# Gate rows fetched from DRAM by broadcast reads, and the row term of a decay exponent given as an activation's bias

## The chip, the cores and the metric

The kernel runs on one core of a Trainium2 chip. The metric is device time in microseconds (us); three timed runs of the kernel before gave 1290.67, 1292.27 and 1293.1, median 1292.27. The trace and its page come from one more execution, taken by the hardware profiler. Engines are named as the profile names them: PE (TensorE matmul), PEld (TensorE weight load), DVE (VectorE), ACT (ScalarE), POOL (GpSimd), SP (SyncE, which here only issues DMAs); ACTq and SPq are the sequencers of ACT and SP, where DMAs are issued.

## The reference, cut to what matters

One transformer-like layer over 1024 tokens of width 1024: an input projection, two mixers side by side, an output projection, a SwiGLU FFN and a gated extra input. The change concerns the second mixer (mLSTM, four heads, chunks; the kernel uses 128 tokens for a chunk). With `ig` and `lf` the input gate and log forget gate, each one number per token and head, the step of a chunk is, cut down:

```python
g = jnp.cumsum(lf, axis=-1)
dmat = g[..., :, None] - g[..., None, :] + ig[..., None, :]     # [t, s], s <= t
m_inter = g + m_st[..., None]
m_t = jnp.maximum(m_inter, jnp.max(dmat, -1))
w_intra = jnp.exp(dmat - m_t[..., None])
w_inter = jnp.exp(m_inter - m_t)
qk = jnp.einsum('bhtd,bhsd->bhts', q_, k_) * w_intra
num = qk @ v_ + w_inter[..., None] * (q_ @ C_st)
```

The exponent of `w_intra` is a sum of a number that depends on s alone (`ig - g` at s) and one that depends on t alone (minus a running maximum at t). With s on partitions and t along a row, the first is one number per partition, and the second is one row that all partitions share. `w_inter` too is one row per head, by which q (head dimension on partitions, t along the row) is multiplied.

## The kernel before

Every large product is made of three fp32r products of split operands (helper `mm3`, lines 86, 87 and 88); the split is a CAST on ACT (line 81) and a subtraction on DVE (line 82). PE does them one after another through the whole kernel.

The stretch that the change touches is early. After a first pass over x (`tok`), four tiles of the convolution (`f_tile(8 + j, conv_evac)`, j = 0 to 3) are multiplied, each in two halves b = 0 and 1 of 24 products of 512 columns into a PSUM bank `ft`. There are two `ft` banks, so a half can only start when ACT has emptied the bank of the half before the last one: `upad<-ft` at line 368. Behind it come four DVE operations (lines 370 and 372), then a Silu on ACT (line 374) and a DMA.

Meanwhile the gates are prepared with 32 rows (8 chunks x 4 heads) on partitions: `ar` is the number per s, `mc` the running maximum per t, `mt` and `wi` further gate rows (lines 288 to 322). To bring row t of a head to all 128 partitions, the kernel before lets PE do it. `stacked` splits a row into a high and a low half, 64 partitions together. For each of the 8 chunks, DVE makes `rd` (line 337), PE makes two products of 512 columns and 64 rows into a bank `pd` (lines 340 and 341), whose sum is the whole exponent; DVE takes the minimum with the causal mask into `Eall` (line 343) and ACT takes one Exp of 128x512 (line 344). In `mlstm(c)`, four products of 64 rows and 128 columns (line 430, `pw`) spread `wi` over 64 partitions each, from where `qw` (line 431) and `wold` (line 432) read it. The small tiles share three banks `ml`.

The chunks of the mLSTM (`mlstm`, a generator) and of the other mixer (`hgrn`) are advanced in steps (`pump`) between the products of the projection tiles. The order on each engine is set by the framework's scheduler, not by the order of the code alone: products of `pd` stand between products of `ft`. Each engine runs its own list in order; a DMA waits at the head of SP's or ACT's list until what it reads is there. The weights are loaded through SP (`wraw`, two buffers).

Of the kernel before, what the change touches and what calls it, by code (L numbers as in the profile page):

```python
# [18 lines left out]
P = 128  # L19
# [15 lines left out]
NH = NC * 4  # L35
# [13 lines left out]
@with_exitstack  # L49
def block_kernel(ctx, tc, a, out):  # L50
    g = Ctx()
    g.tc, g.nc, g.a, g.out = tc, tc.nc, a, out
    nc = tc.nc
    g.act, g.dve, g.pool, g.pe, g.sp = nc.scalar, nc.vector, nc.gpsimd, nc.tensor, nc.sync

    consts = ctx.enter_context(tc.tile_pool(name="consts", bufs=1))
    dram = ctx.enter_context(tc.tile_pool(name="dram", bufs=1, space=DRAM))
    xt = ctx.enter_context(tc.tile_pool(name="xt", bufs=4))
    mp = ctx.enter_context(tc.tile_pool(name="mp", bufs=16))

# [12 lines left out]

    def big(name):
        return xt.tile([P, KT, HB], F32R, tag="big", bufs=4, name=name)

    def mtile(name):
        return mp.tile([P, HB], F32, tag="m", bufs=16, name=name)

    def split(hi, lo, raw):  # L80
        g.act.copy(hi, raw)  # L81
        g.dve.tensor_sub(lo, raw, hi.bitcast(F32))  # L82

    def mm3(acc, lhs, rhs, first, last, more=False):
        (lh, ll), (rh, rl) = lhs, rhs
        g.pe.matmul(acc, lh, rh, start=first, stop=False, skip_group_check=more)  # L86
        g.pe.matmul(acc, lh, rl, start=False, stop=False, skip_group_check=more)  # L87
        g.pe.matmul(acc, ll, rh, start=False, stop=last, skip_group_check=more)  # L88

    def weights(pool_, width, nraw, nhl):  # L90
        def wtile(src, n=1024):
            raw = pool_.tile([P, width], F32, name="wraw", bufs=nraw)
            g.sp.dma_start(raw[:, :n], src)
            hl = pool_.tile([P, 2, width], F32R, name="whl", bufs=nhl)
            hi, lo = hl[:, 0], hl[:, 1]
            split(hi[:, :n], lo[:, :n], raw[:, :n])
            return hi, lo
        return wtile

    g.const, g.big, g.mtile, g.split, g.mm3, g.weights = const, big, mtile, split, mm3, weights  # L100
    g.m8 = consts.tile([P, 8], F32)
    g.dve.memset(g.m8, -0.5)

    def ln_rows(y, p_):
        st = p_.tile([P, 2, 6], F32, name="st6")
        for s in range(2):
            g.dve.bn_stats(st[:, s], y[:, s * HB:(s + 1) * HB])
        mv = p_.tile([P, 4], F32, name="mvs")
        g.dve.bn_aggr(mv[:, 0:2], st)
        ve, rs = mv[:, 2:3], mv[:, 3:4]  # L110
        g.dve.tensor_scalar(ve, mv[:, 1:2], LN_EPS, None, op0=OP.add)
        g.pool.tensor_tensor(rs, ve, g.m8[:, :1], op=OP.pow)
        g.dve.tensor_scalar(y, y, mv[:, 0:1], rs, op0=OP.subtract, op1=OP.mult)

    g.ln_rows = ln_rows
    g.mix = {}
    g.mp = mp
    with tc.tile_pool(reuse_waits="tile", name="wp", bufs=3) as wp:
        g.wp = wp
        g.wtile = weights(wp, 1056, 2, 3)  # L120
        with ExitStack() as es:
            mixers(g, es)
        ff = ExitStack()
        g.psC = ctx.enter_context(tc.tile_pool(reuse_waits="tile", name="psC", bufs=8, space=PSUM))
        g.fw = ff.enter_context(tc.tile_pool(reuse_waits="tile", name="fw", bufs=3, side="right"))
        g.fh = ff.enter_context(tc.tile_pool(reuse_waits="tile", name="fh", bufs=3, side="right"))
        g.fe = ff.enter_context(tc.tile_pool(reuse_waits="tile", name="fe", bufs=8, side="right"))
        with ExitStack() as es:
            out_proj(g, es)
    with ff:  # L130
        with ExitStack() as es:
            ffn_up(g, es)
    with ExitStack() as es:
        ffn_down(g, es)


def mixers(g, es):
# [6 lines left out]
    def bank(tag, shape, name):  # L144
        return ps.tile(shape, F32, tag=tag, bufs={"ft": 2, "hg": 3, "ml": 3}[tag], name=name)
# [23 lines left out]
    for k in range(KT):  # L169
        kk, q = divmod(k, 4)  # L170
# [108 lines left out]
    def srow(nm, dt=F32, n=NH):  # L279
        return kc.tile([n, P], dt, name=nm)  # L280

    ones = srow("ones", n=2 * NH)
    dve.memset(ones, 1.0)
    pgt = bank("ml", [P, 2, P], "pg")
    for i, nm in enumerate(("ig", "lf")):
        pe.transpose(pgt[0:NH, i], sm[nm].rearrange("p c h -> p (c h)"), ident)
    gg, ar, mc, mt, wi = (srow(nm) for nm in ("gg", "ar", "mc", "mt", "wi"))
    dve.tensor_tensor_scan(gg, ones[0:NH], pgt[0:NH, 1], 0.0, op0=OP.mult, op1=OP.add)
    dve.tensor_sub(ar, pgt[0:NH, 0], gg)
    dve.tensor_tensor_scan(mc, ar, ar, NEG, op0=OP.max, op1=OP.max)  # L290
    pl = bank("ml", [P, 2, NH], "pl")
# [13 lines left out]
    dve.tensor_scalar(mprev[:, 1:2], mc[:, P - 1:P], -1.0, None, op0=OP.mult)  # L305
    dve.tensor_add(mt, gg, mc)

    def stacked(nm, src, neg):
        t2 = kc.tile([2 * NH, P], F32R, name=nm)
        if neg:  # L310
            dve.tensor_scalar(t2[0:NH], src, -1.0, None, op0=OP.mult)
            dve.scalar_tensor_tensor(t2[NH:], src, -1.0, t2[0:NH].bitcast(F32), op0=OP.mult, op1=OP.subtract)
        else:
            dve.tensor_copy(t2[0:NH], src)
            dve.tensor_sub(t2[NH:], src, t2[0:NH].bitcast(F32))
        return t2

    m2 = stacked("m2", mc, True)
    a2 = stacked("a2", ar, False)
    act.activation(mt, mt, AF.Exp, scale=-1.0)  # L320
    act.activation(wi, mc, AF.Exp, bias=mprev[:, 0:1], scale=-1.0)
    act.activation(ar, ar, AF.Exp, bias=mprev[:, 1:2], scale=1.0)
    w2 = stacked("w2", wi, False)
    pc = bank("ml", [P, 2, NH], "pc")
    for i, src in enumerate((ar, mt)):
        pe.transpose(pc[:, i], src, ident[0:NH, 0:NH])
    cols = kc.tile([P, 2, NH], F32)
    dve.tensor_copy(cols, pc)
    eyer = kc.tile([2 * NH, NH], F32R)
    dve.tensor_copy(eyer, eye[0:2 * NH])  # L330
    onesr = srow("onesr", F32R, 2 * NH)
    dve.tensor_copy(onesr, ones)
    Eall = kc.tile([P, NC, 4, P], F32)
    for c in range(NC):
        cc = slice(4 * c, 4 * c + 4)
        rd = mx.tile([2 * NH, 4, P], F32R, name="rd", bufs=1)
        dve.tensor_mul(rd, m2.bitcast(F32)[:, None, :].to_broadcast([2 * NH, 4, P]),
                       eye[0:2 * NH, cc, None].to_broadcast([2 * NH, 4, P]))
        pd = bank("ml", [P, 4, P], "pd")
        pe.matmul(pd, a2, eyer[:, cc, None].to_broadcast([2 * NH, 4, P]), start=True, stop=False)  # L340
        pe.matmul(pd, onesr, rd, start=False, stop=True)
        E = Eall[:, c]
        dve.tensor_tensor(E, pd, causal[:, None, :].to_broadcast([P, 4, P]), op=OP.min)
        act.activation(E, E, AF.Exp)

    nfb = kc.tile([P, 4], F32)
    dve.tensor_scalar(nfb, fbias[:, 0:4], -1.0, None, op0=OP.mult)
# [69 lines left out]
    def mlstm(c):  # L417
# [2 lines left out]
        v = mx.tile([P, 4, VW], F32, name="mv")  # L420
        sp.dma_start(v[:, :, 0:P], g.mv_d[c].rearrange("p (h d) -> p h d", h=4))
        dve.memset(v[:, :, P:VW], 1.0)
        pw = bank("ml", [P, 2, 2, P], "pw")
        qw = mx.tile([P, 2, P], F32, name="qw", bufs=1)
        wold = mx.tile([P, 2], F32, name="wold")
        for q in range(2):
            pr = slice(64 * q, 64 * q + 64)
            for p in range(2):
                hc = 4 * c + 2 * p + q
                pe.matmul(pw[:, q, p], eyer[:, hc:hc + 1].to_broadcast([2 * NH, P]), w2, start=True, stop=True)  # L430
            dve.scalar_tensor_tensor(qw[pr], qk[pr, 0:2], 0.125, pw[pr, q], op0=OP.mult, op1=OP.mult)
            dve.tensor_copy(wold[pr], pw[pr, q, :, P - 1])
        E = Eall[:, c]
        for q in range(2):
            pr = slice(64 * q, 64 * q + 64)
# [6 lines left out]
        for p in range(2):  # L442
            pe.transpose(pk[:, p], qk[:, 2 + p], ident)
        kws = mx.tile([P, 4, 64], F32, name="kws", bufs=1)
        dve.tensor_mul(kws, pk.rearrange("p a (b d) -> p (a b) d", b=2),
                       cols[:, 0, 4 * c:4 * c + 4, None].to_broadcast([P, 4, 64]))
        yield
        views = []
        den = mx.tile([P, 4], F32, name="den")
# [10 lines left out]
        for q in range(2):  # L460
            pn = pns[q]
            dn = den[:, q::2]
            dve.tensor_max(dn, pn[:, :, P], cols[:, 1, 4 * c + q:4 * c + 4:2])
            dve.scalar_tensor_tensor(dn, pn[:, :, P], -1.0, dn, op0=OP.mult, op1=OP.max)
            views.append((slice(q, 4, 2), pn[:, :, 0:P]))
        dve.reciprocal(den, den)
# [694 lines left out]
```

## Time and profile before

| | us |
|---|---|
| median of three timed runs | 1292.27 |
| the profiled execution, whole time | 1293.18 |
| its span, first to last instruction | 1291.4 |
| PE busy | 1272.6 (99%) |
| DVE busy | 870.3 (67%) |
| ACT busy | 445.7 (35%) |
| DMA, mean | 148 GB/s |

Between the span and the whole time lie 1.8 us in which the profile shows no instruction. A matmul's bar in the trace is longer than the distance to the next matmul's start, since matmuls are pipelined: the cost of one is read from start to start, not from the length of its bar. A busy share of 99% therefore hides small delays between products.

### The profile page before, as it was taken

Reading aid. Unit: us, or ns where it says so; the run is one execution under the profiler, and the core shown is the slowest. Engines: PE = TensorE matmul, PEld = TensorE weight load, DVE = VectorE, ACT = ScalarE, POOL = GpSimd, SP = SyncE. Lnnn points to the kernel's source line nnn. Section 1 sums busy time; section 2 is a strip of 40 time slices with the busy share of each in tenths; the row PEclk is TensorE's granted clock in tenths of the full one; section 3 lists DMA queues with packets and bytes.
Section 4 is the critical chain, followed back from the end, with each engine's and each line's share of the span. In section 5 each row is a group of like instructions: output and inputs, shape, how many; then the busy total and the mean of one; then the engine's idle time right before and its main releaser. Section 6 shows DMA issues by size and latency. Waiting matters only on the chain.

```text
span 1291.4 us, 19316 instructions
## 1 busy us (share of the span) xinstructions
PE 1272.6 (99%) x7842; PEld 1050.6 (81%) x7842; DVE 870.3 (67%) x1475; ACT 445.7 (35%) x632; POOL 28.4 (2%) x38
## 2 busy tenths in 40 slices
PE   9999999999999999999999999999999999999998
PEld 8689888877788787787788888888888888888887
DVE  7763666466732654478887787787767884559965
ACT  4631312233322514373333333333323433434141
POOL 0000000000000000000000000000000000000000
PEclk9999999999999999999999999999999999999999
DMA  7244321210111745524644433543538876654432
GB/s 246 79 129 130 99 75 34 75 42 26 52 33 49 262 178 179 204 93 146 211 158 175 159 146 143 188 178 123 188 114 308 320 254 198 216 180 153 172 132 74
DMA packets 86472, 191.17 MB, mean 148 GB/s; under 512 B 8304, under 2 KB 26608, under 8 KB 80624
## 3 DMA queue, kind: packets, MB, share of 16 engines
q1 hardware_dynamic: 52112, 130.95, 30.2%
q10 hardware_dynamic: 34272, 59.00, 12.3%
q8 instruction: 61, 1.00, 0.3%
q14 instruction: 27, 0.22, 0.1%
HBM read 139.32 MB, written 50.59 MB: 147 GB/s over the span
## 4 chain that ended last, share of the span: by engine, by line
PE 92%; DVE 5%; ACT 1%; issue 1%; POOL 1%; DMA 0%; ACTq 0%; SPq 0%; POOLq 0%
PE ft L86 8%; PE ft L87 7%; PE ft L88 7%; PE z L86 3%; PE z L88 3%; PE z L87 3%; PE x L86 3%; PE x L88 3%; PE x L87 3%; PE y L86 3%; PE y L88 3%; PE y L87 3%; PE dna L87 2%; PE dna L86 2%; PE pg L86 2%; PE pg L88 2%
## 5 line engine op out<-in xcount | busy, mean ns | idle before, releaser
L86 PE MATMUL ft<-xh,whl 128*128 128x512 f32 x320 | 129.8, 406 | 1.0 <-ACT k L503 1.0
L88 PE MATMUL ft<-xh,whl 128*128 128x512 f32 x320 | 127.8, 399 | 0.0
L87 PE MATMUL ft<-xl,whl 128*128 128x512 f32 x320 | 127.4, 398 | 0.0
L82 DVE TENSOR_TENSOR whl<-hw,whl 128x2048 fp32r<-128x2048 f32 (+1 forms) x42 | 88.4, 2107 | 54.9 <-ACT whl L81 54.9
L81 ACT CAST whl<-hw 128x2048 fp32r<-128x2048 f32 (+1 forms) x42 | 74.2, 1771 | 116.9 <-PE dna L88 41.4
L82 DVE TENSOR_TENSOR whl<-wraw,whl 128x1024 fp32r<-128x1024 f32 x62 | 75.2, 1219 | 40.7 <-ACT whl L81 40.5
L81 ACT CAST whl<-wraw 128x1024 fp32r<-128x1024 f32 x62 | 64.7, 1051 | 107.9 <-PE wo L88 43.8
L81 ACT CAST hl<-gu 128x1024 fp32r<-128x1024 f32 (+1 forms) x48 | 46.8, 981 | 82.9 <-PE x L88 66.9
L86 PEld LDWEIGHTS ft<-xh,whl 128*128 128x128 f32 x320 | 60.8, 190 | 15.7 <-ACT k L503 1.5
L88 PEld LDWEIGHTS ft<-xh,whl 128*128 128x128 f32 x320 | 60.1, 188 | 14.4 <-issue 1.8
L87 PEld LDWEIGHTS ft<-xl,whl 128*128 128x128 f32 x320 | 60.2, 188 | 12.0 <-issue 0.7
L86 PE MATMUL x<-XS,hl 128*128 128x512 f32 x176 | 68.6, 390 | 0.6 <-DVE p L873 0.6
L86 PE MATMUL z<-XA,hl 128*128 128x512 f32 x176 | 68.7, 390 | 0.0
L87 PE MATMUL x<-XS,hl 128*128 128x512 f32 x176 | 68.5, 389 | 0.0
L88 PE MATMUL x<-XS,hl 128*128 128x512 f32 x176 | 68.5, 389 | 0.0
L87 PE MATMUL z<-XA,hl 128*128 128x512 f32 x176 | 68.5, 389 | 0.0
L88 PE MATMUL dna<-whl 128*128 128x512 f32 x176 | 68.5, 389 | 0.0
L86 PE MATMUL dna<-whl 128*128 128x512 f32 x176 | 68.5, 389 | 0.0
L87 PE MATMUL dna<-whl 128*128 128x512 f32 x176 | 68.5, 389 | 0.0
L88 PE MATMUL z<-XA,hl 128*128 128x512 f32 x176 | 68.0, 389 | 0.0
L82 DVE TENSOR_TENSOR hl<-gu,hl 128x1024 fp32r<-128x1024 f32 (+1 forms) x48 | 54.2, 1133 | 7.2 <-ACT hl L81 7.2
L81 ACT CAST hl<-tt 128x1024 fp32r<-128x1024 f32 (+1 forms) x44 | 36.9, 838 | 55.7 <-PE w L88 26.7
(304 smaller groups left out, 3079.9 us busy)
## 6 DMA issues: line engine op xcount, KB each, us to landing
gu<-in_wgu SPq DMA_DIRECT2D x26, 1024.0 KB, 4.9
hw<-h_d SPq DMA_DIRECT2D x35, 512.0 KB, 4.1
wdp<-in_wd SPq DMA_DIRECT2D x11, 1024.0 KB, 5.0
h_d<-hs ACTq DMA_DIRECT2D x44, 256.0 KB, 3.6
wraw<-in_wf SPq DMA_DIRECT2D x20, 512.0 KB, 3.6
hw<-w_d SPq DMA_DIRECT2D x20, 512.0 KB, 4.9
w_d<-wdp ACTq DMA_DIRECT2D x33, 256.0 KB, 3.5
wraw<-in_wo SPq DMA_DIRECT2D x16, 512.0 KB, 3.4
```

The source lines that it names most:

```text
L81: g.act.copy(hi, raw)
L82: g.dve.tensor_sub(lo, raw, hi.bitcast(F32))
L86: g.pe.matmul(acc, lh, rh, start=first, stop=False, skip_group_check=more)
L87: g.pe.matmul(acc, lh, rl, start=False, stop=False, skip_group_check=more)
L88: g.pe.matmul(acc, ll, rh, start=False, stop=last, skip_group_check=more)
```

## The change

Two small DRAM tensors are added. ACT's queue writes the 32x128 rows `wi` and the negated `mc` there. A helper `spread` issues DMAs on SP that read a row with a step of 0 over the partitions, so that each partition gets the same row. `Eall` of a chunk is loaded so with four rows (512 numbers on each of 128 partitions); DVE adds the causal mask; ACT takes the Exp head by head, 128x128 each, with a column of `cols` (the transposed `ar`) as its bias, 32 in all. In `mlstm`, `wb` (two DMAs per chunk, two buffers) replaces `pw`; `qw` becomes one DVE operation over 128 partitions, and `wold` one copy. `stacked`, `rd`, `eyer`, `onesr` and the products at lines 340, 341 and 430 are gone; a third transpose of 32 columns (`pc`) is added.

```diff
+    g.wi_d = dram.tile([NH, P], F32, name="wi_d")
+    g.m_d = dram.tile([NH, P], F32, name="m_d")
...
-    m2 = stacked("m2", mc, True)
-    a2 = stacked("a2", ar, False)
+    pc = bank("ml", [P, 3, NH], "pc")
+    pe.transpose(pc[:, 0], ar, ident[0:NH, 0:NH])
     act.activation(mt, mt, AF.Exp, scale=-1.0)
     act.activation(wi, mc, AF.Exp, bias=mprev[:, 0:1], scale=-1.0)
+    act.dma_start(g.wi_d, wi)
+    dve.tensor_scalar(mc, mc, -1.0, None, op0=OP.mult)
+    act.dma_start(g.m_d, mc)
     act.activation(ar, ar, AF.Exp, bias=mprev[:, 1:2], scale=1.0)
-    w2 = stacked("w2", wi, False)
...
+    def spread(dst, src, r0, rows):
+        ap = [[0, dst.shape[0]], [rows * P, dst.shape[1]], [1, P]]
+        sp.dma_start(dst, bass.AP(tensor=src.tensor, offset=src.offset + r0 * P, ap=ap))
     for c in range(NC):
-        rd = mx.tile([2 * NH, 4, P], F32R, name="rd", bufs=1)
-        dve.tensor_mul(rd, m2.bitcast(F32)[:, None, :].to_broadcast([2 * NH, 4, P]),
-                       eye[0:2 * NH, cc, None].to_broadcast([2 * NH, 4, P]))
-        pd = bank("ml", [P, 4, P], "pd")
-        pe.matmul(pd, a2, eyer[:, cc, None].to_broadcast([2 * NH, 4, P]), start=True, stop=False)
-        pe.matmul(pd, onesr, rd, start=False, stop=True)
         E = Eall[:, c]
-        dve.tensor_tensor(E, pd, causal[:, None, :].to_broadcast([P, 4, P]), op=OP.min)
-        act.activation(E, E, AF.Exp)
+        spread(E, g.m_d, 4 * c, 1)
+        dve.tensor_add(E, E, causal[:, None, :].to_broadcast([P, 4, P]))
+        for h in range(4):
+            act.activation(E[:, h], E[:, h], AF.Exp, bias=cols[:, 0, 4 * c + h:4 * c + h + 1], scale=1.0)
...
-        pw = bank("ml", [P, 2, 2, P], "pw")
+        wb = mx.tile([P, 2, P], F32, name="wb")
+        for q in range(2):
+            spread(wb[64 * q:64 * q + 64], g.wi_d, 4 * c + q, 2)
         qw = mx.tile([P, 2, P], F32, name="qw", bufs=1)
+        dve.scalar_tensor_tensor(qw, qk[:, 0:2], 0.125, wb, op0=OP.mult, op1=OP.mult)
         wold = mx.tile([P, 2], F32, name="wold")
-        for q in range(2):
-            pr = slice(64 * q, 64 * q + 64)
-            for p in range(2):
-                hc = 4 * c + 2 * p + q
-                pe.matmul(pw[:, q, p], eyer[:, hc:hc + 1].to_broadcast([2 * NH, P]), w2, start=True, stop=True)
-            dve.scalar_tensor_tensor(qw[pr], qk[pr, 0:2], 0.125, pw[pr, q], op0=OP.mult, op1=OP.mult)
-            dve.tensor_copy(wold[pr], pw[pr, q, :, P - 1])
+        dve.tensor_copy(wold, wb[:, :, P - 1])
```

The scheduler moves instructions with it. On PE, in the second convolution tile (j = 1, b = 0), the kernel before has `pd` between the products of `ft` from here on:

```order
L326 MATMUL pc<-c_ident,ar 128x32
L326 MATMUL pc<-c_ident,mt 128x32
L340 MATMUL pd<-eyer,a_496 128x512
L341 MATMUL pd<-rd,onesr 128x512
L340 MATMUL pd<-eyer,a_496 128x512
L88 MATMUL ft<-xh,whl 128x512
L86 MATMUL ft<-xh,whl 128x512
L340 MATMUL pd<-eyer,a_496 128x512
```

The changed kernel, at the same place (its lines are shifted: 88 to 90 are `mm3`):

```order
L319 MATMUL pc<-c_ident,ar 128x32
L319 MATMUL pc<-c_ident,mt 128x32
L89 MATMUL ft<-xl,whl 128x512
L90 MATMUL ft<-xh,whl 128x512
L88 MATMUL ft<-xh,whl 128x512
```

All 16 `pd` products are gone from the row of `ft` products, which now runs unbroken to the end of the convolution.

On ACT, the kernel before takes the Exps of `Eall` in groups of one to three, with an emptying of an `ft` bank (`upad<-ft`) between them (here from the gate rows to the second of these emptyings):

```order
L322 ACTIVATE ar<-ar,mprev 32x128
L81 CAST whl<-wraw 128x1024
L374 ACT_TABLE_LOAD
L374 ACTIVATE st<-st 128x512
L344 ACT_TABLE_LOAD
L344 ACTIVATE Eall<-Eall 128x512 x2
L375 DMA mq_d<-st 128x4x128
L368 ACTIVATE upad<-ft,c_fbias 128x512
L344 ACTIVATE Eall<-Eall 128x512 x3
L81 CAST whl<-wraw 128x1024
L344 ACTIVATE Eall<-Eall 128x512
```

The changed kernel, from the same place, has both new writes and then one block:

```order
L317 ACTIVATE ar<-ar,mprev 32x128
L316 DMA m_d<-mc 32x128
L363 ACT_TABLE_LOAD
L363 ACTIVATE st<-st 128x512
L357 ACTIVATE upad<-ft,c_fbias 128x512
L364 DMA mq_d<-st 128x4x128
L83 CAST whl<-wraw 128x1024
L333 ACT_TABLE_LOAD
L333 ACTIVATE Eall<-Eall,cols 128x128 x32
L363 ACT_TABLE_LOAD
L363 ACTIVATE st<-st 128x512
L357 ACTIVATE upad<-ft,c_fbias 128x512
```

All 32 Exps now stand in one piece between two emptyings of `ft` banks (that of j = 1, b = 0, and that of j = 1, b = 1), with a table load and a Silu behind them.

On SP, at the loads of the projection weights, the changed kernel has:

```order
L95 DMA wraw<-in_wf 128x1024 x4
L95 DMA wraw<-in_wt 128x1024
L325 DMA wb<-wi_d 64x2x128 x2
L325 DMA Eall<-m_d 128x512 x8
L325 DMA wb<-wi_d 64x2x128 x2
L95 DMA wraw<-in_wt 128x1024
```

The last load stood directly behind the one of the second row before; it now waits behind twelve reads of the two new tensors.

## Rows read from the trace of the kernel before

**Rows 1.** The page's first part: span and busy time of each engine.

```profile
span 1291.4 us, 19316 instructions
PE 1272.6 (99%) x7842; PEld 1050.6 (81%) x7842; DVE 870.3 (67%) x1475; ACT 445.7 (35%) x632; POOL 28.4 (2%) x38
```

**Rows 2.** PE in two stretches of the convolution (window: its length, PE busy us, matmuls started; granted clock; DMA share and GB/s): three halves with the work of `pd` between them, then three halves without.

```profile
41.00:67.87 26.87, 26.87 (x95) 1.00 0.16 47
67.87:84.60 16.73, 16.73 (x73) 1.00 0.41 124
```

**Rows 3.** PE in order of time (start us, length us, engine, line, operation, output<-inputs, form, count): first products of j = 1, b = 0, then the run around two `pd` products.

```profile
41.02 0.40 PE L86 MATMUL ft<-xh,whl 128*128 128x512 f32 x1
41.34 0.22 PE L301 MATMUL pm<-ones,mrow 1*32 1x1 f32 x2
41.49 0.50 PE L87 MATMUL ft<-xl,whl 128*128 128x512 f32 x1
...
53.84 0.40 PE L88 MATMUL ft<-xh,whl 128*128 128x512 f32 x1
54.16 0.48 PE L340 MATMUL pd<-eyer,a 64*128 64x512 f32 x1
54.58 0.50 PE L86 MATMUL ft<-xh,whl 128*128 128x512 f32 x1
54.91 0.40 PE L87 MATMUL ft<-xl,whl 128*128 128x512 f32 x1
```

**Rows 4.** The same view where `pw` stands: alone between `ft` products (the last product of j = 2, b = 0, the pair, the first of j = 2, b = 1), in a cluster of small products, and split up.

```profile
67.12 0.40 PE L88 MATMUL ft<-xh,whl 128*128 128x512 f32 x1
67.45 0.43 PE L430 MATMUL pw<-w,eyer 64*128 64x128 f32 x2
67.88 0.50 PE L86 MATMUL ft<-xh,whl 128*128 128x512 f32 x1
68.21 0.39 PE L87 MATMUL ft<-xl,whl 128*128 128x512 f32 x1
...
110.15 0.44 PE L430 MATMUL pw<-w,eyer 64*128 64x128 f32 x2
110.43 0.71 PE L438 MATMUL pq<-mqk 64*128 64x128 f32 x8
...
123.63 0.32 PE L430 MATMUL pw<-w,eyer 64*128 64x128 f32 x1
123.66 0.37 PE L438 MATMUL pq<-mqk 64*128 64x128 f32 x1
123.79 0.27 PE L430 MATMUL pw<-w,eyer 64*128 64x128 f32 x1
123.88 0.49 PE L438 MATMUL pq<-mqk 64*128 64x128 f32 x3
```

**Rows 5.** ACT in order of time, the gate rows and the second emptying (in brackets idle time before, and what ended it), and four 128x128 copies without a bias.

```profile
43.27 0.40 ACT L321 ACTIVATE wi<-mc,mprev 32x128 f32<-32x128 f32 x1
43.57 0.29 ACT L320 ACTIVATE mt<-mt 32x128 f32<-32x128 f32 x1
43.77 0.39 ACT L322 ACTIVATE ar<-ar,mprev 32x128 f32<-32x128 f32 x1
44.07 1.03 ACT L81 CAST whl<-wraw 128x1024 fp32r<-128x1024 f32 x1
45.11 1.28 ACT L374 ACT_TABLE_LOAD   x1
46.41 0.63 ACT L374 ACTIVATE st<-st 128x512 f32<-128x512 f32 x1
...
67.16 0.67 ACT L368 ACTIVATE upad<-ft,c_fbias 128x512 f32<-128x512 f32 x1
...
135.68 0.77 ACT L481 COPY mix<-pt 128x128 f32<-128x128 f32 x4 [5.76 <-PE pt L478]
```

**Rows 6.** DVE: when the gate row `mt` is made (timeline), and length of an instruction (ns, least/median/most, first and last start us) at the lines of the mask and of the convolution.

```profile
42.51 0.27 DVE L306 TENSOR_TENSOR mt<-gg,mc 32x128 f32<-32x128 f32 x1
...
L343 DVE TENSOR_TENSOR Eall<-pd,c_causal x8: 676/692/692, 46.6 to 65.9; 128x512 f32<-128x512 f32 x8
...
L372 DVE SCALAR_TENSOR_TENSOR st<-upad,c_convw,st x24: 733/752/753, 36.3 to 89.2; 128x512 f32<-128x512 f32 x24
```

**Rows 7.** DMA issues (queue, count, KB each, median us from issue to landing) and one issue on SP's sequencer (start, length). `btok`, `ln1b` and `ln2g` are rows read from DRAM with a step of 0 over 128 partitions.

```profile
mqk<-mq_d SPq DMA_DIRECT2D x8, 256.0 KB, 2.7
...
ln1b<-in_ln1b SPq DMA_DIRECT2D x1, 512.0 KB, 7.1
ln2g<-in_ln2g SPq DMA_DIRECT2D x1, 512.0 KB, 14.4
...
btok<-in_btok SPq DMA_DIRECT2D x1, 256.0 KB, 4.8
...
c_lbl<-in_lbl SPq DMA_DIRECT2D x1, 4.0 KB, 2.0
...
20.00 0.43 SPq L71 DMA_DIRECT2D c_ln1c<-in_ln1c  x1
```

**Rows 8.** PE in two stretches later in the kernel (columns as in rows 2): one with waits in it, and the one behind it.

```profile
537.00:540.44 3.44, 1.78 (x7) 1.00 0.73 284
540.44:543.86 3.42, 3.42 (x10) 0.50 0.81 302
```

More of the change, by code (lines that the diff above doesn't have):

```diff
@@ L280, in srow @@
         return kc.tile([n, P], dt, name=nm)
-    ones = srow("ones", n=2 * NH)
+    ones = srow("ones")
     dve.memset(ones, 1.0)
@@ L287, in mixers @@
     gg, ar, mc, mt, wi = (srow(nm) for nm in ("gg", "ar", "mc", "mt", "wi"))
-    dve.tensor_tensor_scan(gg, ones[0:NH], pgt[0:NH, 1], 0.0, op0=OP.mult, op1=OP.add)
+    dve.tensor_tensor_scan(gg, ones, pgt[0:NH, 1], 0.0, op0=OP.mult, op1=OP.add)
     dve.tensor_sub(ar, pgt[0:NH, 0], gg)
@@ L306, in mixers @@
     dve.tensor_add(mt, gg, mc)
[L308 to L316, printed above, removed]
-    m2 = stacked("m2", mc, True)
-    a2 = stacked("a2", ar, False)
+    pc = bank("ml", [P, 3, NH], "pc")
@@ L320, in mixers @@
+    pe.transpose(pc[:, 0], ar, ident[0:NH, 0:NH])
     act.activation(mt, mt, AF.Exp, scale=-1.0)
     act.activation(wi, mc, AF.Exp, bias=mprev[:, 0:1], scale=-1.0)
+    act.dma_start(g.wi_d, wi)
+    dve.tensor_scalar(mc, mc, -1.0, None, op0=OP.mult)
+    act.dma_start(g.m_d, mc)
     act.activation(ar, ar, AF.Exp, bias=mprev[:, 1:2], scale=1.0)
-    w2 = stacked("w2", wi, False)
-    pc = bank("ml", [P, 2, NH], "pc")
     for i, src in enumerate((ar, mt)):
-        pe.transpose(pc[:, i], src, ident[0:NH, 0:NH])
@@ L327, in mixers @@
-    cols = kc.tile([P, 2, NH], F32)
+        pe.transpose(pc[:, 1 + i], src, ident[0:NH, 0:NH])
+    cols = kc.tile([P, 3, NH], F32)
     dve.tensor_copy(cols, pc)
[L329 to L332, printed above, removed]
+    def spread(dst, src, r0, rows):
+        ap = [[0, dst.shape[0]], [rows * P, dst.shape[1]], [1, P]]
+        sp.dma_start(dst, bass.AP(tensor=src.tensor, offset=src.offset + r0 * P, ap=ap))
@@ L333, in mixers @@
     Eall = kc.tile([P, NC, 4, P], F32)
     for c in range(NC):
-        cc = slice(4 * c, 4 * c + 4)
-        rd = mx.tile([2 * NH, 4, P], F32R, name="rd", bufs=1)
-        dve.tensor_mul(rd, m2.bitcast(F32)[:, None, :].to_broadcast([2 * NH, 4, P]),
-                       eye[0:2 * NH, cc, None].to_broadcast([2 * NH, 4, P]))
-        pd = bank("ml", [P, 4, P], "pd")
-        pe.matmul(pd, a2, eyer[:, cc, None].to_broadcast([2 * NH, 4, P]), start=True, stop=False)
-        pe.matmul(pd, onesr, rd, start=False, stop=True)
@@ L445, in mlstm @@
         dve.tensor_mul(kws, pk.rearrange("p a (b d) -> p (a b) d", b=2),
-                       cols[:, 0, 4 * c:4 * c + 4, None].to_broadcast([P, 4, 64]))
+                       cols[:, 1, 4 * c:4 * c + 4, None].to_broadcast([P, 4, 64]))
         yield
@@ L462, in mlstm @@
             dn = den[:, q::2]
-            dve.tensor_max(dn, pn[:, :, P], cols[:, 1, 4 * c + q:4 * c + 4:2])
+            dve.tensor_max(dn, pn[:, :, P], cols[:, 2, 4 * c + q:4 * c + 4:2])
             dve.scalar_tensor_tensor(dn, pn[:, :, P], -1.0, dn, op0=OP.mult, op1=OP.max)
```

## The prediction

> **What bounds the kernel now.** I read the page's first part, then windows by stage, then PE's timeline, and last ACT's and DVE's around it. PE is busy for 99% of the span [rows 1], so the time falls only if PE has less to do or waits less; the reader should then distrust the 99%, because bars overlap. The windows show what they hide. Three halves of the convolution without the gate work (67.87 to 84.60) are 16.73 us with 73 matmuls, 0.229 us each; the three halves before them (41.00 to 67.87) hold the same 72 large products and take 26.87 us [rows 2]. So the stretch with `pd` in it is 10.1 us longer. PE's timeline shows how: from the `ft` product at 53.84 to the next at 54.58 it is 0.74 us instead of 0.23, and the one behind needs 0.33, so one `pd` product costs 0.61 us although it computes as many columns as an `ft` product [rows 3]. Switching between 64 and 128 rows costs as much as the work. The 16 of them at 0.61 would be 9.8; as some stand side by side I go by the stretch: 10.1, less 0.6 for the one lone `pw` pair in it (67.12 to 67.88 is 0.76 instead of 0.23, the next start 0.10 late) [rows 4] and some 0.6 for the transposes and `pm` that stay, which leaves 8.9.
>
> **What goes, part by part.** *PE, `pd`:* 8.9 us of PE's list, and 0.6 for the lone `pw` pair. *PE, the other 15 `pw` pairs:* in a cluster a pair holds the products behind it up by 0.28 us (110.15 to 110.43); where the scheduler split it, the two parts hold up 0.03 and 0.09 [rows 4]. Bounds for 15: 1.8 and 4.2, or 9.5 if each cost what the lone one did; I take 0.24 each, near the plain cluster, 3.6 us. PE is the bound there, so this counts in full. *DVE:* `rd`, `stacked` and one of two `qw` operations per chunk go; DVE does not bound here, worth nothing by itself. The mask costs what it did (0.69) [rows 6].
>
> **What comes, and where it decides.** The `ft` products now run unbroken, but each half needs a bank that ACT must empty, and all 32 Exps stand between the emptying of j = 1, b = 0 and that of j = 1, b = 1. So I follow that list.
>
> - PE: j = 1, b = 0 starts at 41.02 as before [rows 3]; 24 products at 0.23 and about 0.8 for `pm` (0.34 from 41.02 to 41.49 beyond a product's distance, less what the first product takes) and three transposes end it near 47.6. The next half needs 5.5 more, the one after that (into the bank emptied near 48.3) ends at 58.7. Its successor, j = 2, b = 1, wants the bank of j = 1, b = 1.
> - The row: `mt` is made at 42.51 to 42.78; then three convolution operations of 0.72 and the negation of 0.27 [rows 6] give `mc` at 45.2. ACT writes it (a small DMA lands after 2.0), SP issues the first `Eall` at 47.3; it lands 2.6 later as `mqk`, 256 KB, does: 49.9 [rows 7]. Eight issues at 0.4 to 0.7 put the last landing near 54. DVE reaches the first mask only after the convolution operations ahead of it: 51.2.
> - ACT: after the write at 45.2 (0.35) a table load 1.28, Silu 0.63, emptying 0.67 (47.6 to 48.3), a DMA issue 0.37, a CAST 1.03, a table load 1.28: ready at 51.0 [rows 5]. Queue, DVE and ACT thus meet within 1.5 us of each other.
> - 32 Exps with a bias: the trace has no 128x128 one. The 32-row ones of the same row length: with a bias they last 0.39 to 0.40, and the next starts 0.30 later (43.27 to 43.57, 43.77 to 44.07); without, 0.29 and 0.20. Four copies without a bias take 0.77, so 0.165 each [rows 5]. Bounds 0.165 and 0.40, that is 5.3 and 12.8 us; I take 0.30, the row with a bias: 9.6. They end at 60.9; DVE's masks (8 x 0.69 and the split of a weight) are done near 58 and don't bind.
> - Then table load 1.28, Silu 0.63, emptying 0.67: the bank is free at 63.5. PE, done at 58.7, waits 4.8 us. Before, j = 2, b = 1 began at 67.88 [rows 4]. Gain here: 4.4 of the 9.5 that left PE's list. The rest waits on ACT.
>
> The queue of SP: what stands behind the broadcasts are the weights of the second `tok_group`, wanted past 80; ACT's and DVE's lists behind the Exps run some 2 us ahead of PE's next need. I count them at nothing; the cover is gone if the Exps end 3 us later. The reads of `wb` wait for the buffer of two chunks earlier, as `mqk` does; nothing.
>
> **The clock.** A wait of this kind has a second price. In a stretch of 3.44 us in which PE was busy for 1.78, the granted clock was still 1.00; in the next 3.42 it was 0.50, that is 1.2 instead of 2.4 GHz, and PE made 10 matmuls in it [rows 8] where 15 fit at 0.229. That is 1.1 to 1.6 us lost. A wait of 4.8 us is longer than the 1.66 idle in that stretch, so I add one such loss, 1.6; bounds are nothing (the low clock lies inside the wait) and two, 3.2. The Trainium skill (TensorE: Matmul & The Clock Gate, Why this matters for your kernels) says the same as a rule: keep PE free of idle gaps between bursts, or its clock falls back to the low level. That rule speaks against this change, and rows 8 bear it out; no wait as long stands in this trace. Without it the sum below would be 1.6 better.
>
> **The sum.** Against the profiled execution, 1293.18 (span 1291.4 and 1.8 around it): 4.4 - 1.6 + 3.6 = 6.4 us less, 1286.8. The median shown is 0.9 under that execution, so the like median is 1285.9; I say 1286.0. Behind the mixers nothing is touched, and PE's list there just starts earlier.
>
> **Rivals.**
> 1. *The block is short, PE does not wait for ACT* (20%). If an Exp starts each 0.165, DVE's masks bind, the block ends near 58.9, the bank is free at 61.5, PE waits 2.8 and the clock may hold: 6.4 + 3.6 = 10.0 less, 1282. For it: the copies in rows 5. Against: the rows with a bias.
> 2. *The block is long or late, the stage gives nothing* (20%). At 0.40 the Exps end at 64.0, the bank at 66.6; with 1.6 to 3.2 for the clock the stage loses 0.3 to 1.9, and `pw` alone is left: 1.7 to 3.3 less, 1289 to 1291. A landing 3 us later does the same. For it: three chains meet within 1.5 us, and any delay of one moves the block. Against: each has its own row.
> 3. *The broadcasts are slow, and the kernel becomes slower* (8%). Rows read with step 0 over the partitions landed 7.1 and 14.4 us after issue for 512 KB, 4.8 for 256 KB [rows 7], up to three times a plain read. If 256 KB each take 3.5 us one after another, eight take 28: the last lands at 75.5, masks, Exps, table, Silu and emptying put the bank at 80, 12 us after 67.88; with the clock 13.7, less 3.6: 10 slower, 1302. It decides once the last row lands after 65, eleven us later than I reckon. Against: those reads stood in line with weight loads, when DMA was far busier than the 47 GB/s of this stretch [rows 2].
> 4. *The change doesn't do what it says* (2%): PE would still hold products at the lines that go. The order excludes it; what is left is any upset of later stages by the new order.
>
> **How the numbers follow.** Forecast 50%, rivals 20, 20, 8, 2. The forecast's own range, from an Exp distance 0.27 to 0.33 and a clock loss of 0 to 3.2, with 0.2 to 0.28 for a `pw` pair, is 1283.5 to 1288.5. To leave out no more than 2 in 10 I go to 1281.5 on rival 1's side and to 1291 on rival 2's. About 0.2% (2.6 us: 1289.7 and 1294.9) is what a measurement can tell. Faster: the forecast, rival 1 and a fifth of rival 2, 0.74; same: the rest of rival 2 and half of rival 4, 0.17; slower: rival 3 and the rest, 0.09.
>
> **What would show it.** In the trace of the changed kernel: no `pd`, no `pw`; `ft` products 0.23 apart from 47 to 58; 32 Exps of some 0.39 us starting each 0.30, first near 51; PE idle for some 5 us before j = 2, b = 1, ended by ACT's `upad`, with a granted clock of 0.5 for about 3.4 us at its end; that half starting near 63.5. If PE does not wait there, rival 1 holds; if the idle time is ended by a landing of `Eall` through DVE, rival 3 or 2. If the stretch from there to the last step of the mLSTM has not become 3 to 4 us shorter, the `pw` term is wrong.

## The result, and the profile after

The changed kernel takes 1283.94 us (median of four runs, 1282.37 to 1285.11), the kernel before 1291.94 in the same comparison: ratio 0.9938, 95% interval 0.9920 to 0.9955, so 8.0 us less. Its profiled execution took 1282.37 us. Two of the four runs took 1282.4 and 1282.8 us at a mean granted clock of 0.998 and 0.997, the other two 1285.1 at 0.995, so they spent longer at the low clock than the execution that the trace shows.

The first part of its page answers to [rows 1]; the last two lines are from the costliest groups and the DMA issues:

```profile
span 1280.6 us, 19251 instructions
PE 1257.1 (98%) x7795; PEld 1043.4 (81%) x7795; DVE 857.4 (67%) x1444; ACT 448.3 (35%) x654; POOL 28.4 (2%) x38
...
L88 PE MATMUL ft<-xh,whl 128*128 128x512 f32 x320 | 129.9, 406 | 5.9 <-ACT upad L357 4.9
...
Eall<-m_d SPq DMA_DIRECT2D x8, 256.0 KB, 5.8
```

PE now has idle time, and one line names it: 4.9 us before an `ft` product, ended by ACT's emptying `upad`. ACT's timeline between the two emptyings (as rows 5) shows what it was doing instead:

```profile
48.04 0.69 ACT L357 ACTIVATE upad<-ft,c_fbias 128x512 f32<-128x512 f32 x1 [0.28 <-PE ft L90]
48.10 0.39 ACTq L364 DMA_DIRECT2D mq_d<-st  x1
48.62 1.04 ACT L83 CAST whl<-wraw 128x1024 fp32r<-128x1024 f32 x1
49.68 1.28 ACT L333 ACT_TABLE_LOAD   x1
51.84 9.56 ACT L333 ACTIVATE Eall<-Eall,cols 128x128 f32<-128x128 f32 x32 [0.87 <-DVE Eall L331]
61.42 1.28 ACT L363 ACT_TABLE_LOAD   x1
62.72 0.63 ACT L363 ACTIVATE st<-st 128x512 f32<-128x512 f32 x1
63.25 0.67 ACT L357 ACTIVATE upad<-ft,c_fbias 128x512 f32<-128x512 f32 x1
```

PE's timeline at that place, and behind it windows of two and four us (window: its length; busy us and instructions of PE, PEld, DVE, ACT and POOL; granted clock; DMA share and GB/s):

```profile
58.70 0.40 PE L90 MATMUL ft<-xh,whl 128*128 128x512 f32 x1
63.97 0.67 PE L88 MATMUL ft<-xh,whl 128*128 128x512 f32 x1 [4.87 <-ACT upad L357]
```

The windows:

```profile
60.00:64.00 4.00, 0.03 (x1) 0.03 (x1) 0.04 (x1) 3.97 (x9) 0.00 (x0) 1.00 0.00 1
64.00:66.00 2.00, 2.00 (x5) 1.62 (x6) 1.93 (x4) 0.86 (x1) 0.00 (x0) 0.54 0.50 139
66.00:68.00 2.00, 2.00 (x7) 1.53 (x7) 1.88 (x4) 0.09 (x1) 0.00 (x0) 0.61 0.00 0
68.00:70.00 2.00, 2.00 (x10) 1.66 (x9) 0.85 (x3) 1.12 (x2) 0.00 (x0) 1.00 0.55 154
```

The clock was granted in full while PE stood still; it fell to 0.50 (1.2 of 2.4 GHz) as PE started again, for 3.41 us (64.14 to 67.55), and PE made 5 and 7 products in windows where it makes 10.

To see where the time went, I compare two places that every kernel of this study has: A, the first 256-column product of the second token group, right behind the convolution, and B, the first `pkt` product, behind the last step of the mLSTM. The median is of the timed runs, and the ratio is to the kernel before timed beside that version (its medians: 1291.65 to 1292.37). A and B are from the traces, one execution each, in us. The first half of the convolution starts between 28.4 and 29.5 in them, so A and B alone carry up to 1.1 us that no edit made; B - A does not:

| kernel | median | ratio, 95% | A | B | B - A |
|---|---|---|---|---|---|
| before | 1291.94 | | 84.63 | 223.80 | 139.17 |
| changed | 1283.94 | 0.9938 (0.9920 to 0.9955) | 82.29 | 215.41 | 133.12 |
| `w_only` | 1287.05 | 0.9962 (0.9950 to 0.9975) | 85.88 | 219.24 | 133.36 |
| `e_only` | 1291.28 | 0.9994 (0.9985 to 1.0003) | 84.46 | 223.59 | 139.13 |
| `pw_dbl` | 1292.82 | 1.0009 (1.0000 to 1.0018) | 84.69 | 225.13 | 140.44 |
| `pw_full` | 1293.20 | 1.0010 (1.0001 to 1.0020) | 84.58 | 224.25 | 139.67 |
| `pw_hg` | 1289.50 | 0.9978 (0.9969 to 0.9987) | 85.13 | 221.21 | 136.08 |
| `fill` | 1281.49 | 0.9920 (0.9907 to 0.9934) | 81.10 | 214.21 | 133.11 |
| `e_late` | 1286.49 | 0.9964 (0.9950 to 0.9977) | 75.82 | 218.92 | 143.10 |
| `exp_one` | 1281.05 | 0.9916 (0.9901 to 0.9930) | 80.11 | 213.32 | 133.21 |
| `exp_in` | 1277.33 | 0.9886 (0.9872 to 0.9901) | 76.56 | 210.25 | 133.69 |

The changed kernel gains 2.34 us to A and 6.05 from A to B; 0.6 is lost again between 257 and 264 us of the kernel before (the gain falls from 8.39 to 7.81; the cause stays open), which leaves 7.8 beside the timed 8.0. The spans differ by 10.8, since the one profiled execution of the kernel before has two delays that are not the change's: at the low clock of [rows 8] the gain steps from 7.78 to 9.35, and at a wait of PE of 1.24 us at 602 to 10.95. The trace of `pw_dbl`, which touches nothing there, has neither; that of `pw_full` has the first.

### The profile page after: what moved, and what is told of

It is laid out like the page before. It is cut to its first block, busy times and chain, and to the rows that moved or that the text cites. A ratio compares the mean times of both kernels' runs of the same rounds, so it can differ in the third digit from the quotient of the medians.

```text
span 1280.6 us, 19251 instructions
## 1 busy us (share of the span) xinstructions
PE 1257.1 (98%) x7795; PEld 1043.4 (81%) x7795; DVE 857.4 (67%) x1444; ACT 448.3 (35%) x654; POOL 28.4 (2%) x38
## 4 chain that ended last, share of the span: by engine, by line
PE 90%; DVE 5%; ACT 2%; issue 1%; DMA 1%; POOL 1%; POOLq 0%; ACTq 0%
PE ft L88 7%; PE ft L89 7%; PE ft L90 7%; PE z L88 3%; PE z L90 3%; PE z L89 3%; PE x L88 3%; PE x L90 3%; PE x L89 3%; PE y L88 3%; PE y L90 3%; PE y L89 3%; PE pg L88 2%; PE dna L89 2%; PE dna L88 2%; PE dna L90 2%
```

## The experiments

### The two parts, each alone

`w_only` is the kernel before with only the `wi` rows read from DRAM; `e_only` is the changed kernel with the `pw` products put back.

```diff
--- before
+++ w_only
...
-        pw = bank("ml", [P, 2, 2, P], "pw")
+        wb = mx.tile([P, 2, P], F32, name="wb")
+        for q in range(2):
+            spread(wb[64 * q:64 * q + 64], g.wi_d, 4 * c + q, 2)
...
--- changed
+++ e_only
...
-        wb = mx.tile([P, 2, P], F32, name="wb")
+        pw = bank("ml", [P, 2, 2, P], "pw")
...
```

> Only the wi rows go through DRAM (wb); the pd products and the Exps of 512 stay as in the kernel before. Theory 1: the two parts of the change add up, and the mLSTM's steps get from this part alone the 6.0 us that the trace of the changed kernel shows between the end of the convolution and the last mLSTM step, besides 0.6 for the lone pw pair in the convolution: about 6 us under the kernel before. Rival: a pw pair costs 0.24 as predicted and the other 2.4 us come from the earlier end of the Exps or of the convolution: about 4 us under, and the mLSTM stretch 3.6 shorter.

> Only Eall is fetched from DRAM, with the bias in the Exp; pw stays. Theory 1: the convolution ends some 2 us earlier than in the kernel before (2.65 less the 0.6 of the lone pw pair), the mLSTM steps take what they took: about 2 us under the kernel before, PE idle for some 5 us before the fourth half of the convolution and a stretch of low clock behind it. Rival: the stage is worth nothing without the other part, 0 us.

Measured: 4.6 us less for `w_only`, 0.4 (not different from nothing) for `e_only`. From A to B, `w_only` alone has 5.81 of the 6.05 us and `e_only` none: the surplus over the forecast belongs to the `pw` part (products, their bank and what reads them). At A `w_only` is 1.25 later, of which 0.27 is its later start; in the convolution PE waits 1.62 us for ACT ahead of j = 2, b = 1. And `e_only` gains nothing there: that half's emptying comes still later (64.89, behind all 32 Exps again), since in its order ACT takes a Silu and a CAST ahead of the block, which starts at 55.53 instead of 51.84. So the rival's 0 us came and not the theory's 2, by the placing of the block; the parts do not simply add up. PE's timeline at these waits, first of `w_only`:

```profile
69.14 0.50 PE L87 MATMUL ft<-xh,whl 128*128 128x512 f32 x1 [1.62 <-ACT upad L373]
```

That of `e_only`, and the window with the low clock:

```profile
58.61 0.43 PE L430 MATMUL pw<-w,eyer 64*128 64x128 f32 x2
65.61 0.80 PE L87 MATMUL ft<-xh,whl 128*128 128x512 f32 x1 [6.57 <-ACT upad L368]
```

```profile
63.39:70.22 6.83, 4.61 (x11) 3.65 (x12) 3.26 (x6) 4.66 (x10) 0.00 (x0) 0.50 0.03 10
```

A wait of 6.57 us, and a low clock for 6.83 us, twice as long as in the changed kernel: all that left PE's list there was given back in one place. Here the clock fell 2.2 us before PE started again (63.39 and 65.61). Behind the wait of `w_only` it stayed at 1.00.

### What a `pw` pair costs

The forecast took a pair by its place in PE's list. Two tests of other prices: each product twice, and the products over 128 rows, half of them zero.

```diff
--- before
+++ pw_dbl
             for p in range(2):
                 hc = 4 * c + 2 * p + q
-                pe.matmul(pw[:, q, p], eyer[:, hc:hc + 1].to_broadcast([2 * NH, P]), w2, start=True, stop=True)
+                for _ in range(2):
+                    pe.matmul(pw[:, q, p], eyer[:, hc:hc + 1].to_broadcast([2 * NH, P]), w2, start=True, stop=True)
--- before
+++ pw_full
-    w2 = stacked("w2", wi, False)
+    w2 = kc.tile([P, P], F32R, name="w2")
+    dve.tensor_scalar(w2, ident, 0.0, None, op0=OP.mult)
+    dve.tensor_copy(w2[0:NH], wi)
+    dve.tensor_sub(w2[NH:2 * NH], wi, w2[0:NH].bitcast(F32))
...
-    eyer = kc.tile([2 * NH, NH], F32R)
+    eyer = kc.tile([P, NH], F32R)
...
```

> The kernel before, with each of the 32 small products that spread the gate rows over partitions in the mLSTM (the pw products) issued twice into the same place, the second over the first. Three prices stand against each other. If a pair costs its place in PE's list, at the forecast's 0.24 us: 16 more pairs cost 3.8, 1295.5 us. If it costs in the list what its removal gave back (5.8 to 6.05 us over 16 pairs, 0.37 us a pair): 5.9 more, 1297.6. If the price sits in what stands around a pair (the turn from 128 rows to 64 and back, or VectorE's work and waits behind it), which a second product beside the first does not pay again: at most 16 x 0.11 = 1.8 more, 1291.9 to 1293.5.

> The kernel before, with the pw products over 128 rows instead of 64: the two operands are filled up with zero rows, all else is as it was. If a good part of a pair's price is the turn between products over 128 rows and products over 64, the stretch from 84.6 to 223.7 us becomes shorter by up to 6.0 less the products' own time (16 x 0.11 = 1.8), so up to 4 us: 1287.5 to 1290. If the price is the list's (each small product at its length) or VectorE's behind it, nothing changes: 1291.7, within 0.5.

Doubling cost 0.8 us (1.27 from A to B, 0.08 a pair), within the third price and far from 3.8 or 5.9: what a pair's removal gave back does not grow with the number of products. It doesn't price a product either, since part of the doubled ones fell into a wait that is there anyway: in the third chunk the second half of `pq` starts 1.13 us behind the last `pt` product with them and 1.14 without. The wider products brought nothing (0.5 us longer from A to B): the turn from 128 to 64 rows is not saved, only moved. In the third chunk `pw` starts 0.03 us behind `pt` instead of 0.21, and `pq` 0.20 behind `pw` instead of 0.11. PE's timeline of `pw_dbl` says more:

```profile
122.51 0.66 PE L431 MATMUL pw<-w,eyer 64*128 64x128 f32 x4
123.01 0.66 PE L439 MATMUL pq<-mqk 64*128 64x128 f32 x4
123.59 0.39 PE L86 MATMUL ft<-whl,xh 128*128 128x256 f32 x1
...
124.15 0.32 PE L431 MATMUL pw<-w,eyer 64*128 64x128 f32 x1
124.16 0.37 PE L439 MATMUL pq<-mqk 64*128 64x128 f32 x1
...
124.80 0.44 PE L444 MATMUL pk<-c_ident,mqk 128*128 128x128 f32 x2
```

In the first group four `pw` and then four `pq` take 1.08 us to the next product. In the second the same eight take 0.65, and `pw` and `pq` start 0.01 us apart. There `pw` is multiplied over rows 0 to 63 and the `pq` of the second half over rows 64 to 127; in the first group both use rows 0 to 63. Products over different halves of the rows run beside each other. That leads to `pq` itself, whose two halves use different rows. PE's timeline in the third chunk, for the kernel before and behind it the changed kernel:

```profile
135.58 0.43 PE L430 MATMUL pw<-w,eyer 64*128 64x128 f32 x2
135.85 0.43 PE L438 MATMUL pq<-mqk 64*128 64x128 f32 x2
...
136.24 0.65 PE L438 MATMUL pq<-mqk 64*128 64x128 f32 x2
136.59 0.32 PE L430 MATMUL pw<-w,eyer 64*128 64x128 f32 x1
```

The weight loads of the kernel before, at the same place:

```profile
136.51 0.18 PEld L438 LDWEIGHTS pq<-mqk 64*128 64x128 f32 x1 [0.19 <-ACT mix L481]
```

The changed kernel:

```profile
132.05 0.39 PE L424 MATMUL pq<-mqk 64*128 64x128 f32 x2
...
132.05 0.72 PE L424 MATMUL pq<-mqk 64*128 64x128 f32 x8
```

(The first line of the changed kernel's listing is of a narrow window: the first two instructions together last 0.39 us, one alone 0.37. In the first listing the group at 136.24 is the last instruction of the first half and, at 136.51, the first of the second.) In the changed kernel all eight instructions are done in 0.72 us; in the kernel before the second half starts 0.66 us behind the first. So it is in three of its eight chunks; in four the two halves are 0.90 to 1.25 us apart, with other products between them, and only in the first chunk do they run side by side. What ends the wait at 136.51 is ACT's `mix<-pt` at line 481, which empties an `ml` bank (the four copies of [rows 5], done at 136.45). The program's order names the same cause (with buffer numbers, and what an instruction waits for):

```
kernel before
L430 MATMUL pw_1460<-w2_502,eyer_510 128x128 x2
L438 MATMUL pq_1471<-mqk_1455 128x128 [waits DMAHW7_49]
L438 MATMUL pq_1471<-mqk_1455 128x128
L438 MATMUL pq_1475<-mqk_1455 128x128 [waits Activation_49]
changed kernel
L424 MATMUL pq_1444<-mqk_1432 128x128 [waits DMAHW1_49]
L424 MATMUL pq_1444<-mqk_1432 128x128
L424 MATMUL pq_1448<-mqk_1432 128x128 x2
```

Before, the second `pq` tile waits until ACT has emptied an `ml` bank, with `pw` in another of the three; without `pw` it waits for nothing, and the wait for the same copy comes later and shorter, ahead of `pk` (0.21 us at 132.99). So the test is to leave every product in place and take `pw` out of `ml`:

```diff
--- before
+++ pw_hg
-        pw = bank("ml", [P, 2, 2, P], "pw")
+        pw = bank("hg", [P, 2, 2, P], "pw")
```

> The kernel before, with the pw products in a bank of the tag hg instead of ml; products, reads and everything VectorE computes stay. In the trace of the kernel before, the second half of a chunk's pq products (rows 64 to 127) starts behind the first half (rows 0 to 63), 136.51 against 135.85 us, and its wait is for a bank of ml; in the changed kernel, which has no pw in ml, the two halves start 13 ns apart and run beside each other (132.05 and 132.07 us), 8 instructions in the time of 4. If this is what the gain of the pw part had beyond its places in PE's list (theory), 8 chunks x 0.27 to 0.30 us come back without a single product less: the stretch from 84.6 to 223.7 us becomes 2.0 to 2.4 us shorter, 1289.8 us, ratio 0.998. If the gain beyond the forecast came from the products themselves or from VectorE's halved work on them (rival), nothing changes: 1292.1, ratio 1.000.

Measured: ratio 0.9978, 2.9 us less, and 3.09 less from A to B; the trace has the eight `pq` in one piece:

```profile
135.44 0.44 PE L430 MATMUL pw<-w,eyer 64*128 64x128 f32 x2
135.72 0.71 PE L438 MATMUL pq<-mqk 64*128 64x128 f32 x8
```

The theory holds: a good part of the 6.05 us came from a bank, not from work. In `pw_hg` the eight `pq` run in one piece in all eight chunks. But 3.09 is not the bank's alone: the scheduler moved two more pairs ahead of A, so that `pw_hg` has 13 between A and B where the kernel before has 15. Those 13 are what `pw_hg` still lacks of the changed kernel there, 136.08 - 133.12 = 2.96 us or 0.23 each. At that price 15 pairs are 3.4 of the 6.05, and 2.6 are left for the bank, near the expected 2.0 to 2.4. The split is an estimate: 1.0 of the 2.96 is again a wait for a bank (five times `pw` waits for VectorE's `wold` in `hg`), and what VectorE's halved work is worth was not separated from the products.

### The block of Exps

`fill` gives PE something to do in its wait: 20 products that nothing reads. `e_late` writes the loop over `Eall` behind the convolution.

```diff
--- changed
+++ fill
+FILL = 20
...
+            if i == 10 and b == 1:
+                junk = bank("hg", [P, 512], "junk")
+                for _ in range(FILL):
+                    pe.matmul(junk, hi[:, 0], xh[0][:, 0], start=True, stop=True)
--- changed
+++ e_late
     Eall = kc.tile([P, NC, 4, P], F32)
-    for c in range(NC):
-        E = Eall[:, c]
-        spread(E, g.m_d, 4 * c, 1)
...
         f_tile(8 + j, conv_evac, None if j else conv0)
+    for c in range(NC):
+        E = Eall[:, c]
+        spread(E, g.m_d, 4 * c, 1)
...
     tok_group("wt1", 264, g.mv_d, 256)
```

> The changed kernel with 20 products of 512 columns that nothing reads, put into PE's list where it waits (20 at 0.23 are 4.6 us). Theory 1: the half behind the wait starts when ACT has emptied the bank, as before at about 64 us, but at full clock: 1.6 us under the changed kernel, about 1282.3. Rival: the low clock has another cause than this wait: clock 0.5 still stands there, and the time is the changed kernel's or 0 to 1 us more.

> The changed kernel with the loop over Eall written behind the convolution; the scheduler then spreads the 32 Exps over its later halves, a few at a time, with a table load on either side. Theory 1: the 4.9 us that PE waits for the emptying of a bank, and the low clock behind it, come from the block of 32 Exps alone; with the Exps spread both go: 6.4 us under the changed kernel, about 1277.5. Rival: the landing of the broadcasts or the extra table loads hold ACT up in another half, PE waits there as long, and the time stays within 2 us of the changed kernel.

PE's timeline of `fill`, and a window behind it:

```profile
59.61 4.70 PE L261 MATMUL junk<-xh,whl 128*128 128x512 f32 x20
64.35 0.50 PE L89 MATMUL ft<-xh,whl 128*128 128x512 f32 x1
```

```profile
64.00:66.00 2.00, 1.95 (x9) 1.39 (x8) 1.60 (x3) 1.24 (x2) 0.00 (x0) 1.00 0.46 131
```

The half starts 0.38 us later than in the changed kernel (its convolution began 0.53 later), the clock stays at 1.00, and A is reached 1.19 earlier. So the low clock cost 0.38 + 1.19 = 1.57 us, as much as the stretch of [rows 8]. By the medians work without a use makes the kernel 2.4 us faster, 1281.49, though the two ratios' intervals overlap; none of its four runs has a mean clock under 0.999, where two of the changed kernel have 0.995.

In `e_late` the convolution runs unbroken, and A comes 6.47 us earlier than in the changed kernel. Then it is lost again, as PE's timeline and the window around its two waits show:

```profile
82.01 0.81 PE L425 MATMUL pq<-mqk 64*128 64x128 f32 x4 [2.88 <-DMA mqk<-mq_d]
...
86.97 0.79 PE L88 MATMUL ft<-whl,xh 128*128 128x256 f32 x2 [3.11 <-ACT whl L83]
```

```profile
81.46:91.70 10.24, 6.11 (x28) 5.22 (x29) 4.21 (x7) 6.38 (x14) 0.00 (x0) 0.50 0.54 155
```

The scheduler pulled `pq` of the first chunk ahead of a load that had not landed, and left ten Exps ahead of the weight casts that PE needs. Two waits, and 10.24 us at the low clock: B comes 3.51 us later than in the changed kernel, and the median is 2.55 higher (intervals overlap).

Two more versions: one Exp per chunk (without the term of s), and the four Exps written into the chunk's own step, where only the chunk itself needs them.

```diff
--- changed
+++ exp_one
-        for h in range(4):
-            act.activation(E[:, h], E[:, h], AF.Exp, bias=cols[:, 0, 4 * c + h:4 * c + h + 1], scale=1.0)
+        act.activation(E, E, AF.Exp)
--- changed
+++ exp_in
         dve.tensor_add(E, E, causal[:, None, :].to_broadcast([P, 4, P]))
-        for h in range(4):
-            act.activation(E[:, h], E[:, h], AF.Exp, bias=cols[:, 0, 4 * c + h:4 * c + h + 1], scale=1.0)
...
         E = Eall[:, c]
+        for h in range(4):
+            act.activation(E[:, h], E[:, h], AF.Exp, bias=cols[:, 0, 4 * c + h:4 * c + h + 1], scale=1.0)
         for q in range(2):
```

> The changed kernel, with one Exp of 512 columns for each chunk instead of four of 128 with a bias; the term of the decay's position s in the exponent is left out. The block on ScalarE becomes about 8 x 0.6 = 5 us instead of 9.56, and the program's order puts a Silu between the fifth and the sixth Exp. If the block's length makes PE's wait of 4.87 us and the low clock of 3.4 us behind it (theory), both go: the convolution ends 4.9 + 1.5 = 6.4 us earlier, 1277.5 us, and no less than 4 earlier, 1280. If the wait is set by the landing of the rows in DRAM or by the tables that ScalarE loads between Exp and Silu (rival), most of the wait stays: 1282 to 1284.

> The changed kernel, with the four Exps of a chunk written into the chunk's own step of the mLSTM, the broadcast reads and the masks where they were. The program's order has ScalarE take the Exps in groups of 1, 9, 3, 3, 3, 3 and 2 between the convolution's Silus and ten behind the last of them; PE's order stays as in the changed kernel. If the block is all that broke the convolution, and nothing new is late: no wait in the convolution, 6.5 us less than the changed kernel (what the kernel with the late loop had gained at 75 us), 1277.5. If the ten Exps ahead of two weight casts make the token weights late as in that kernel (PE idle 3.1 us, low clock behind it): 3.1 + 2 to 5 are given back, 1283 to 1286.

`exp_one`, 1281.05, lies between its two expectations. PE still waits 2.25 us, and the low clock lasts as long as in the changed kernel (3.41 us). PE's timeline:

```profile
61.80 0.64 PE L88 MATMUL ft<-xh,whl 128*128 128x512 f32 x1 [2.25 <-ACT upad L356]
```

ACT's timeline says why:

```profile
53.24 1.24 ACT L332 ACTIVATE Eall<-Eall 128x512 f32<-128x512 f32 x2 [0.63 <-DVE Eall L331]
54.95 1.30 ACT L332 ACTIVATE Eall<-Eall 128x512 f32<-128x512 f32 x2 [0.48 <-DVE Eall L331]
56.27 1.28 ACT L362 ACT_TABLE_LOAD   x1
57.57 0.63 ACT L362 ACTIVATE st<-st 128x512 f32<-128x512 f32 x1
58.22 1.28 ACT L332 ACT_TABLE_LOAD   x1
59.51 1.67 ACT L332 ACTIVATE Eall<-Eall 128x512 f32<-128x512 f32 x3
61.08 0.67 ACT L356 ACTIVATE upad<-ft,c_fbias 128x512 f32<-128x512 f32 x1
```

With shorter Exps, ACT waits for the masks, and a second pair of table loads stands in between: the emptying comes only 2.2 us earlier. The block's length and what surrounds it share the wait, and neither theory holds alone.

`exp_in`, 1277.33, meets the theory's 1277.5. Its groups between two emptyings are short, as ACT's timeline shows at the longest of them; the listing behind it has PE's longest wait in the convolution:

```profile
57.87 2.75 ACT L419 ACTIVATE Eall<-Eall,cols 128x128 f32<-128x128 f32 x9
60.63 1.28 ACT L361 ACT_TABLE_LOAD   x1
62.21 0.63 ACT L361 ACTIVATE st<-st 128x512 f32<-128x512 f32 x1 [0.29 <-DVE upad L352]
62.75 0.67 ACT L355 ACTIVATE upad<-ft,c_fbias 128x512 f32<-128x512 f32 x1
```

```profile
70.91 0.50 PE L88 MATMUL ft<-xh,whl 128*128 128x512 f32 x1 [0.41 <-ACT upad L355]
```

PE never waits longer than these 0.41 us there, and the clock is 1.00 through all of it, although ACT loads tables eleven times more up to B. The feared lateness of the token weights did not come: from A to B it is 0.57 us behind the changed kernel. It is 6.6 us faster than the changed kernel and 14.7 faster than the one before, the best version of this study.

## Why the prediction was right, and where it was not

1286.0 was said, 1283.94 came; it lies in the range and, 2.1 us under the forecast, in the likeliest case's own range as well (1283.5 to 1288.5), at its edge. The likeliest case is what the trace shows, but that the sum came so near is partly luck: one term missed by 2.4 us, outside its own range, and the spread allowed for the Exps and the clock took it in.

- *The row's way.* First `Eall` issue 47.3 forecast, 46.89 in the trace; first mask 51.2 and 51.11; first Exp 51.3 (60.9 less 9.6) and 51.84, since the sum left out that the first Exp waits for the first mask, 0.69 long. The landing was taken from a plain read, 2.6 us ([rows 7] have 2.7); it is 5.8 (median of eight), but DVE waited for it only 0.6 us in all, since the convolution's operations stand ahead of the first mask. So rival 2's "landing 3 us later" came, and did not give its outcome.
- *The block.* 32 Exps at 0.30 us, 9.6 in all: 9.56. The row with a bias was the right one to go by, and rival 1, from the copies without one, falls.
- *The wait.* 4.8 us from 58.7, half at 63.5: 4.87, 63.97. Two slips cancelled on the way to 58.7: 41.02, 24 products at 0.23 and 0.8 make 47.3 and not 47.6 (and 0.47 from 41.02 to 41.49 is 0.24 beyond a product's distance, not 0.34), but the half took 6.51 us, 1.0 more than its products instead of 0.8.
- *The clock.* One stretch of 3.4 us costing 1.6: 1.57 by `fill`, in the executions traced; by the mean clocks two of the four timed ones had more. The rule of the Trainium skill (TensorE: Matmul & The Clock Gate, Why this matters for your kernels) against gaps between bursts did speak against this change, and the trace agrees: filling the gap is worth 1.57 us in the traces, 2.4 by the medians.
- *The stage.* 2.8 us of gain forecast. A comes 2.34 earlier, in an execution that was 0.35 behind at the convolution's start: 2.7.
- *The `pw` pairs: the mis-sized term.* "I take 0.24 each, near the plain cluster, 3.6 us" came out at 6.05, beyond the 0.2 to 0.28 a pair of the forecast's own range. The prediction named the sign, a stretch not 3 to 4 us shorter. The place of a pair in the list was priced about right (0.23 by `pw_hg`, what VectorE does with it included). What the step left out is that `pw` is also a buffer: it took one of three `ml` banks, and so in seven of eight chunks the second half of `pq` waited for ACT, or was listed behind other products, and could not run beside the first. That is some 2.6 us, by `pw_hg`. The hint stood in [rows 4]: where `pw` is split up, only four `pq` stand (123.66 and 123.88), in the cluster at 110.43 all eight in one piece. I read those rows for how long `pw` holds up its neighbour, and not for what `pq` itself would do without it.
- *Rivals 2 and 3.* A longer wait with twice the low clock does come, in `e_only` (6.57 and 6.83 us, stage gain nothing): rival 2's outcome, by the placing of ACT's work rather than by a longer Exp. Slow broadcasts did not come: the last mask starts at 57.9.

The stage and the clock hit, `pw` missed by 2.4 us in the good direction; the 0.6 us lost behind B stands against it.

## What to carry to other kernels

A tile that is removed frees its buffer too: look for the instruction behind it that waits for a bank, and price that wait by itself. When work moves from the bound engine to another, ask between which of that engine's duties it lands; here the same 32 Exps as one block between two emptyings made the kernel 6.6 us slower than in groups of up to nine, and writing them where they are needed was enough to have the scheduler spread them. An idle gap of the matmul engine can be paid twice, once as the wait and once at the low clock behind it (here with the waits of 2.25 us and more, not with the 1.62 of `w_only`), and a version that only moves the gap, as `e_late`, pays again.

## What was not expected of the hardware

- Two 64-row products on different halves of the rows run beside each other: eight instructions in 0.72 us where four over one half take 0.66 (`pw_dbl`, 123.01). The Trainium skill (TensorEngine Tiling (Array Packing), Key Properties) says that different tiles can load weights and multiply in parallel; the traces agree, and the weight load at 136.51 and `pw_hg` show besides that a bank wait between the two undoes it.
- The low clock lasted 3.41 us at waits of 4.87 and of 2.25 us, 6.83 at one of 6.57, 10.24 at 2.88 and 3.11 close together: not in proportion to the wait. Nor does the wait alone decide. PE's wait of 1.13 us for `pp` that ends at 538.46 in the kernel before, 2 us ahead of the low clock of [rows 8], stands in all eleven traces, and the low clock follows it in two (kernel before and `pw_full`).
- A broadcast read of 256 KB lands late, 5.8 us after its issue beside 2.7 for a plain one [rows 7], yet eight in a row are not slow: issued from 46.89 to 51.1, they were all there when the last mask started at 57.9, and from 52 to 56 us the DMA engines moved 383 GB/s on the mean. Eight landings added up one behind the other, as rival 3 had them, are no price. How much of the 5.8 is the step of 0 and how much the seven others was not separated.
